# Fixed PSUM banks in the attention stage of a hybrid attention and Fourier block

## The chip, the cores and the metric

The kernel runs on one core of a Trainium2 chip. The metric is the device time of one execution in microseconds (us). The kernel before takes 612.53 us, the median of three runs (611.64, 612.53 and 614.63). The execution that was profiled took 611.92 us; its trace spans 610.1 us, and the other 1.8 us lie around the span.

## The reference

One layer of a backbone over 1024 latent tokens of width 1024, with 256 context tokens ahead of them as a prefix. One input projection feeds two groups: latent attention with 8 heads (low-rank queries and keys, a rotary part of 32), and a two-dimensional Fourier mixing followed by a linear map. The two are gated, concatenated and multiplied with one output matrix; a layer norm closes the layer. Cut to what matters here:

```python
h_x = _layer_norm(x) * (1.0 + scale_x) + shift_x
qlat_x, ckv_x, krope_x, gmla_x, fin_x, gf_x = _split_proj(h_x, w_in, b_in)
# per head (8 heads, 1024 queries, 1280 keys, 96 wide; values 64 wide)
s = einsum("bqhd,bkhd->bhqk", q, k) / sqrt(QK_DIM)
p = softmax(s, axis=-1)
attn_x = einsum("bhqk,bkhv->bqhv", p, v)
four_x = fft2(fin_x, axes=(1, 3)).real @ w_fourier + b_fourier
y = concatenate([attn_x * silu(g_mla), four_x * silu(g_f)]) @ w_out + b_out
x_new = _layer_norm(DEEPNORM_ALPHA * x + gate_x * y, post_ln_g, post_ln_b)
```

## The kernel before

The span has three parts. Up to about 283 us TensorE (PE) does the input projection, the query and key preparation and the Fourier transform. From 283 to about 505 us the attention loop runs, and from there to 602 us the output product with the layer norm behind it; the last 8 us are the layer norm's end.

Numbers are kept in two pieces, a high and a low one, so a product is three matmuls (h times h, h times l, l times h), and each tile that is read out of PSUM is read twice: ACT copies the high piece (`evac`, L774), and DVE subtracts it from the PSUM value to get the low piece (L776, L778). The PSUM bank is free only after the DVE readout.

The attention works on 32 pairs of 128-row query tiles (8 heads, 4 pairs each), a pair in about 7 us. Iteration n of the loop does the scores of pair n+1 (PE into SL0, SL1 and SC), their row minimum (DVE, E), the exponential (ACT, E), the split into a high (ACT, L1046) and a low piece (POOL, L1054; together EH), and the DMA transpose of both (ET<-EH), and for the pair of two iterations earlier the products with V (`pv`, PE, L1096 and L1099). The product is read out by ACT (pvt, L1105) and DVE (at, L1115). On all engines the loop's order is written out (SEQ). "f" in SEQ is a slot for a filling task of that iteration: building queries of the next head (`build_qt`, tile qh), keys (`build_kt`, kt), values (`build_v`, v), or the finish of two heads: `finish_rows` spreads the reciprocals of the row sums over 64 columns on POOL (rb, L1134), and `finish_pair` transposes them on PE (r, L1142) and scales the gate with them on DVE. `S0a` and `S0b` are parts of the scores, `P0` and `P1` the halves of the products with V. The last pairs transpose their weights on PE instead (et, `e_tr` and `e_out`).

PSUM has eight banks here: SL0 and SL1 take two each, SC one, and three rotate under the name "tr" for all that `tr(...)` allocates: qh, kt, v, r, pv, et and o. A new tile takes the bank of the oldest and waits for its readout.

In the output stage tiles t = 0 to 7 of 128 rows are accumulated over 8 blocks k; t = 0 and 1 (and 4, 5) go into SL0 and SL1, the others into SC and "tr" tiles (`po_t`: o20, o2512, o3, o60, ...; o70 is the first half of tile 7). `out_mms` issues the matmuls (L1193), and `finish` (DVE) multiplies with the gate (y, L1401), adds the residual (xr, L1402), takes the statistics (L1403, L1405), and scales (L1417, L1421). Outside the loop a scheduler orders the instructions of each engine when the program is built.

Of the kernel before, what the change touches and what calls it, by code (L numbers as in the profile page):

```python
# [11 lines left out]
F32 = mybir.dt.float32  # L12
# [7 lines left out]
PSUM = bass.MemoryType.PSUM  # L20

P = 128
# [30 lines left out]
FT = eval("{'k': [-1, 0, 1], 'q': [1, 2], 'r': 4, 'p': [6, 7], 'v': [13, 15, 15, 16, 17], 'g': 33}")  # L53
# [11 lines left out]
def tile_hybrid_block(ctx: ExitStack, tc: tile.TileContext, a, out, dbg=None):  # L65
# [11 lines left out]

    pools = {}

    def tr(name):  # L80
        return pools["tr"].tile([P, 512], F32, tag="tr", name=name)

    def split(hi, lo, src, eng=None):
        nc.gpsimd.tensor_scalar(out=hi, in0=src, scalar1=1.0, scalar2=0.0, op0=ALU.mult, op1=ALU.add)
        (eng or nc.vector).tensor_tensor(out=lo, in0=src, in1=hi.bitcast(F32), op=ALU.subtract)

    rest = []

    def hi_v(hi, lo, src):
# [616 lines left out]
    with tc.manual_schedule(engines={ET.PE}):  # L706
# [5 lines left out]
        pt = tr("cktc")  # L712
# [93 lines left out]

    V = {}

    def build_v(grp, i2, pool):
        if grp == 0 and i2 % 2 == 0:  # L810
            V[grp, i2 // 2] = u4([P, 2, 2, 4, 2, 64], F16, f"V{grp}{i2}")
        elif i2 == 0:
            v = qpool.tile([P, 5, 2, 4, 2, 64], F16, tag="q", name="V1")
            for i in range(0, 5, 2):
                V[grp, i // 2] = v[:, i:min(i + 2, 5)]
        pt = tr(f"v{grp}{i2}")
        for i in range(2):
            mm3(pt[:, 256 * i:256 * i + 256],
                [(ck(2 * i2 + i, 0), ck(2 * i2 + i, 1), wv[:, 0, 256 * grp:256 * grp + 256],
                  wv[:, 1, 256 * grp:256 * grp + 256])])  # L820
        vt = V[grp, i2 // 2][:, i2 % 2].rearrange("p i h l c -> p (i h) l c")
        evac(vt[:, :, 0, :], vt[:, :, 1, :], pt.rearrange("p (a c) -> p a c", c=64), pool)
# [39 lines left out]
    for par in range(2):  # L862
        pq = []
        for nt in range(4):
# [4 lines left out]
            if par == 1:  # L869
                t = u4([P, 2, 2, 4, 64], F32R, f"pqs{par}{nt}")  # L870
            else:
                if nt % 2 == 0:
                    t2 = pools["e"].tile([P, 2, 2, 2, 4, 64], F32R, tag="ET", name=f"pqs{par}{nt}", bufs=ETB)
                t = t2[:, nt % 2]
            pv = ps.rearrange("p (g t c) -> p t g c", t=2, c=64)
# [75 lines left out]
    def fourier_out(par, m, alloc):  # L951

        AT, BT, NT_ = four[par]
        NK = (258, 256)[par]
        ms = slice(m * P, (m + 1) * P)
        pa, pb = alloc(f"pa{par}{m}"), alloc(f"pb{par}{m}")
        nc.tensor.matmul(pa[:, 0:NK], lhsT=wn[:, 0, ms], rhs=NT_[:, 0:NK], start=True, stop=False)
        mm3(pa[:, 0:NK], [(wp_hi[:, gp, ms], wp_lo[:, gp, ms], AT[:, gp, 0, :], AT[:, gp, 1, :])
                          for gp in range(2)], False)
        mm3(pb[:, 0:NK], [(wm_hi[:, gp, ms], wm_lo[:, gp, ms], BT[:, gp, 0, :], BT[:, gp, 1, :])  # L960
                          for gp in range(2)])
        ta = small.tile([P, 512], F32, tag="h", name="ta", bufs=4)
        nc.scalar.activation(out=ta[:, 0:NK], in_=pa[:, 0:NK], func=AF.Identity, bias=bfo[:, m:m + 1])
        mf = mixf[m]
        if par == 0:
            outs = ((slice(0, 513, 2), 0, 257, ALU.subtract), (slice(1022, 512, -2), 1, 256, ALU.add))
        else:
            outs = ((slice(1, 512, 2), 0, 256, ALU.subtract), (slice(1023, 512, -2), 0, 256, ALU.add))
        for ks, r0, r1, op in outs:
            tf = small.tile([P, 512], F32, tag="h", name="tf", bufs=4)  # L970
            nc.vector.tensor_tensor(out=tf[:, r0:r1], in0=ta[:, r0:r1], in1=pb[:, r0:r1], op=op)
            nc.gpsimd.tensor_tensor(out=mf[:, ks], in0=tf[:, r0:r1], in1=mf[:, ks], op=ALU.mult)
        return ta
# [8 lines left out]
    ps_ctx.close()  # L982
    tr_ctx.close()
    at_ctx = ExitStack()
    pools["tr"] = at_ctx.enter_context(tc.tile_pool(name="ps_tr2", bufs=3, space=PSUM, reuse_waits="tile"))
    ps_s = at_ctx.enter_context(tc.tile_pool(name="ps_s", bufs=1, space=PSUM, reuse_waits="tile"))


# [1 line left out]
    SC = ps_s.tile([P, 512], F32, tag="SC", name="SC")  # L990

    class Pair:
# [91 lines left out]

        def pv(self, kts, first=False, last=False):
            if first:
                self.po = tr("pv")
            po = self.po[:, 0:256]
            tiles = self.ET.rearrange("p j t q -> p (j t) q")
            for hl in range(2):  # L1090
                for kt in kts:
                    v = V[self.grp, kt // 4][:, kt // 2 % 2, kt % 2, self.h % 4]
                    t, d = 10 * hl + kt, 20
                    e = tiles[:, t:t + d + 1:d, :]
                    if hl == 0:
                        nc.tensor.matmul(po, lhsT=v.rearrange("p l c -> p (l c)"), rhs=e, start=(kt == 0), stop=False)  # L1096
                    else:
                        g = kt % 2
                        nc.tensor.matmul(po[64 * g:64 * g + 64], lhsT=v[:, 0], rhs=e, start=False,  # L1099
                                         stop=(kt >= 8), tile_position=(0, 64 * g))  # L1100
# [25 lines left out]
    def finish_rows(pair, half):  # L1126

        rb = small.tile([P, 4, 2, 64], F32, tag="h", name="rb", bufs=4)
        for e in range(2):
            o, i = rb[:, :, e, :], rinv[2 * pair + e][:, 4 * half:4 * half + 4].unsqueeze(2).to_broadcast([P, 4, 64])  # L1130
            if RBE == "a":
                nc.scalar.activation(out=o, in_=i, func=AF.Copy)
            else:
                nc.gpsimd.tensor_scalar(out=o, in0=i, scalar1=1.0, scalar2=0.0, op0=ALU.mult, op1=ALU.add)  # L1134
        rbs[pair, half] = rb

    def finish_pair(pair, half):
        hs = slice(512 * half, 512 * half + 512)
        rb = rbs[pair, half]
        pt = tr(f"r{pair}{half}")  # L1140
        for i in range(4):
            nc.tensor.transpose(pt[:, i * P:(i + 1) * P], rb[:, i].rearrange("p a b -> p (a b)"), ident)  # L1142

        def out():
            nc.vector.scalar_tensor_tensor(out=gm[pair][:, hs], in0=pt, scalar=vscale[:, 0, pair:pair + 1],
                                           in1=gm[pair][:, hs], op0=ALU.mult, op1=ALU.mult)
            {'v': nc.vector, 'p': nc.gpsimd}[GME].tensor_tensor(out=gm[pair][:, hs], in0=ats[pair][:, hs], in1=gm[pair][:, hs], op=ALU.mult)

        on_dve(out)
# [34 lines left out]
    HALVES = ((0, 512), (512, 1024))  # L1184
# [11 lines left out]
    def po_t(t):  # L1196

        if t % 4 < 2:
            return {c: SL[t % 4][:, c[0]:c[1]] for c in HALVES}
        if t % 4 == 2:  # L1200
            return {c: tr(f"o{t}{c[0]}") for c in HALVES}
        return {HALVES[0]: SC, HALVES[1]: tr(f"o{t}")}

    NP = 4 * HEADS
    fills = {n: [] for n in range(NP + LAG)}
# [1 line left out]
    for h in range(HEADS - 1):  # L1207
        if h % 2:
            for c in range(3):
                fills[4 * h + FT['k'][c]].append(lambda c=c, p=(h + 1) // 2: build_kt(p, c, BP))  # L1210
        for hf in range(2):
            fills[4 * h + FT['q'][hf]].append(lambda hf=hf, h1=h + 1: build_qt(h1, hf, BQ))
        if h % 2:
            p = h // 2
            fills[4 * h + FT['r']].append(lambda p=p: (finish_rows(p, 0), finish_rows(p, 1)))
            for hf in range(2):
                fills[4 * h + FT['p'][hf]].append(lambda hf=hf, p=p: finish_pair(p, hf))
    for i, n in enumerate(FT['v']):
        fills[n].append(lambda i=i: build_v(1, i, BV))
# [18 lines left out]
    with tc.manual_schedule(engines={ET.PE}):  # L1238
        VA, VB = eval('(1,3)')
        for i2 in range(VA):  # L1240
            build_v(0, i2, False)
        p0.s_lat(0, 0)
        p0.s_lat(0, 1)
        p0.s_lat(0, 2)
        for i2 in range(VA, VB):
            build_v(0, i2, False)
        if "m0'" not in SEQ:
            p0.max_lat(0)
        if "c0'" not in SEQ:
            p0.max_ctx(0)  # L1250
        if "t0'" not in SEQ:
            p0.bias(0)
        if "x0'" not in SEQ:
            p0.exp(0)
        if "h0'" not in SEQ and not p0.on_pe(0):
            p0.hi(0)
        if "l0'" not in SEQ and not p0.on_pe(0):
            p0.lo(0)
        p0.s_lat(1, 0)
        p0.s_lat(1, 1)  # L1260
        p0.s_lat(1, 2)
        for i2 in range(VB, 3):
            build_v(0, i2, False)
        if "m1'" not in SEQ:
            p0.max_lat(1)
        if "c1'" not in SEQ:
            p0.max_ctx(1)
        if "t1'" not in SEQ:
            p0.bias(1)
        if "x1'" not in SEQ:  # L1270
            p0.exp(1)
        if "h1'" not in SEQ:
            p0.hi(1)
        if "l1'" not in SEQ:
            p0.lo(1)
        for m in range(2, 4):
            fourier_out(1, m, tr)
    for m in range(4):
        dump(f"mixf{m}", mixf[m])

    with tc.manual_schedule(engines={{'P': ET.PE, 'V': ET.DVE, 'A': ET.Activation, 'G': ET.Pool, 'S': ET.SP}[c] for c in MAN}):
        for n in range(NP + LAG):
            nxt, prv = pairs.get(n + 1), pairs.get(n - LAG)
            h = n // 4
# [233 lines left out]
```

## Time and profile before

| what | value |
|---|---|
| median of three runs | 612.53 us |
| profiled execution; its span | 611.92 us; 610.1 us |
| PE, DVE, ACT, POOL busy | 577.2, 384.4, 310.0, 280.9 us |
| PE's weight loads (PEld) busy | 461.1 us |
| chain that ended last | PE 59%, DMA 14%, DVE 8%, ACT 7%, POOL 4% of the span |

PE is busy for 95% of the span, but matmuls are pipelined and their ends in the trace are modelled, so that figure doesn't say that PE is at its peak. The chain that ended last follows the work back from the last instruction, at each step to what released it. Its shares say which waits matter in which stage; an engine that waits off that chain costs nothing.

### The profile page before, as it was taken

How to read it: one execution, taken by the hardware profiler on the slowest of the kernel's cores; microseconds unless marked ns; L12 is line 12 of the kernel's file. 1: busy time of each engine (PE TensorE's matmuls, PEld its weight loads, DVE VectorE, ACT ScalarE, POOL GpSimd, SP SyncE). 2: the span in 40 equal slices, each digit the busy share in tenths (PEclk: the TensorE clock that was granted, in tenths of full speed). 3: DMA queues.
4: the chain of work that ended last, by engine and by line, in shares of the span. 5: the costliest groups of instructions: out<-in, count | busy, mean ns of one | idle time of the engine just before them, and what ended most of it. 6: DMA issues, size and time to landing. Idle time of an engine off the chain costs nothing.

```text
span 610.1 us, 9587 instructions
## 1 busy us (share of the span) xinstructions
PE 577.2 (95%) x3521; PEld 461.1 (76%) x3521; DVE 384.4 (63%) x878; ACT 310.0 (51%) x484; POOL 280.9 (46%) x220
## 2 busy tenths in 40 slices
PE   8999999999999999999899999999889998999994
PEld 7787777888899999889666676776656666788883
DVE  6438317811003496687776778677757756699897
ACT  3323621211024343467999989889978875600000
POOL 3123215011002349665877887788998851400000
PEclk9999999999999999999999999999999999999998
DMA  9999029000001041212999999999999996520432
GB/s 287 317 307 397 28 70 319 15 1 0 1 0 53 1 130 46 71 44 44 181 194 187 202 184 176 185 173 207 193 180 193 192 214 209 219 92 0 154 123 105
DMA packets 191927, 86.86 MB, mean 142 GB/s; under 512 B 160428, under 2 KB 182188, under 8 KB 191880
## 3 DMA queue, kind: packets, MB, share of 16 engines
q1 hardware_dynamic: 191880, 86.24, 60.4%
q8 instruction: 28, 0.46, 0.3%
q14 instruction: 19, 0.16, 0.1%
HBM read 41.39 MB, written 4.20 MB: 75 GB/s over the span
## 4 chain that ended last, share of the span: by engine, by line
PE 59%; DMA 14%; DVE 8%; ACT 7%; issue 5%; POOL 4%; SPq 2%; DVEq 0%; POOLq 0%; ACTq 0%
DMA ET<-EH 12%; PE g L322 11%; PE SL L1193 7%; PE fin L322 7%; PE o L1193 5%; POOL EH L1054 3%; ACT EH L1046 3%; PE tm L137 2%; PE tm L138 2%; PE tm L139 2%; ACT E L1037 2%; PE pv L1096 2%; DVE E L1018 2%; PE pv L1099 2%; DMA wada<-in_w_ada_dram 1%
## 5 line engine op out<-in xcount | busy, mean ns | idle before, releaser
L1054 POOL TENSOR_TENSOR EH<-E,EH 128x1280 f16<-128x1280 f32 x61 | 160.3, 2633 | 39.4 <-ACT EH L1046 38.2
L1018 DVE TENSOR_SCALAR_CACHE_REDUCE E<-SL 128x1024 f32<-128x1024 f32 x64 | 78.1, 1221 | 24.6 <-POOL EH L1054 20.5
L1046 ACT ACTIVATE EH<-E 128x1280 f16<-128x1280 f32 x61 | 77.4, 1269 | 21.2 <-DMA ET<-EH 20.0
L1037 ACT ACTIVATE E<-E,mx 128x1280 f32<-128x1280 f32 x64 | 86.8, 1356 | 1.5 <-DVE mx L1031 0.9
L322 PE MATMUL fin<-h,wh 128*128 128x512 f32 x192 | 65.0, 406 | 0.0
L322 PE MATMUL g<-h,wh 128*128 128x512 f32 x192 | 60.3, 394 | 1.0 <-DVE upm L384 1.0
L1096 PE MATMUL pv<-ET,V 128*128 128x256 f16 x320 | 45.8, 274 | 14.3 <-DMA ET<-EH 9.4
L137 PE MATMUL SL<-KTh,QT 96*128 96x512 f32 x128 | 55.4, 433 | 0.5 <-ACT QT L774 0.5
L1096 PEld LDWEIGHTS <-V 128*128 128x128 f16 x320 | 26.8, 97 | 36.1 <-issue 26.8
L139 PE MATMUL SL<-KTh,QT 96*128 96x512 f32 x128 | 50.6, 395 | 0.0
L138 PE MATMUL SL<-KTl,QT 96*128 96x512 f32 x128 | 50.4, 394 | 0.0
L322 PEld LDWEIGHTS fin<-h,wh 128*128 128x128 f32 x192 | 35.9, 188 | 10.3 <-issue 2.9
L1018 DVE TENSOR_SCALAR_CACHE_REDUCE E<-SC 128x256 f32<-128x256 f32 x64 | 26.8, 419 | 26.7 <-PE SC L139 26.2
L322 PEld LDWEIGHTS g<-h,wh 128*128 128x128 f32 x192 | 36.0, 188 | 9.8 <-issue 1.4
L353 POOL TENSOR_SCALAR h<-xnT,mod 128x512 f32<-128x512 f32 x15 | 12.8, 854 | 62.4 <-DVE mod L272 29.7
L322 PE MATMUL g<-h,wl 128*128 128x512 f32 x96 | 37.8, 394 | 0.0
L322 PE MATMUL fin<-h,wl 128*128 128x512 f32 x96 | 37.1, 395 | 0.0
L113 ACT ACTIVATE rs_t<-mvf,eps 128x1 f32<-128x1 f32 x8 | 2.4, 295 | 68.1 <-DVE mvf L1405 61.6
L431 ACT ACTIVATE gt<-g,cols 128x512 f32<-128x512 f32 x12 | 8.0, 688 | 56.1 <-PE g L322 56.1
L1415 POOL TENSOR_TENSOR xr<-xr,lng 128x256 f32<-128x256 f32 x2 | 1.4, 726 | 70.7 <-ACT xr L1414 70.7
L1099 PE MATMUL pv<-ET,V 128*64 128x256 f16 x320 | 33.0, 282 | 0.0
L354 DVE TENSOR_TENSOR h<-h,h 128x512 fp32r<-128x512 f32 x15 | 13.6, 905 | 30.0 <-POOL h L353 22.7
(347 smaller groups left out, 1443.4 us busy)
## 6 DMA issues: line engine op xcount, KB each, us to landing
wada<-in_w_ada_dram SPq DMA_DIRECT2D x32, 256.0 KB, 6.0
x<-in_x_dram SPq DMA_DIRECT2D x8, 512.0 KB
wgate<-in_w_ada_dram SPq DMA_DIRECT2D x8, 512.0 KB, 7.5
wor<-in_w_out_dram SPq DMA_DIRECT2D x8, 512.0 KB, 4.0
xr<-in_x_dram SPq DMA_DIRECT2D x8, 512.0 KB, 4.3
out_dram<-xr SPq DMA_DIRECT2D x15, 256.0 KB, 2.1
wr<-in_w_in_dram SPq DMA_DIRECT2D x6, 512.0 KB, 5.4
wtr<-in_w_in_dram SPq DMA_DIRECT2D x4, 416.0 KB, 6.3
```

Of the source, the lines that this page charges most:

```text
L137: nc.tensor.matmul(ps, lhsT=sh, rhs=mh, start=(start and i == 0), stop=False)
L138: nc.tensor.matmul(ps, lhsT=sh, rhs=ml, start=False, stop=False)
L139: nc.tensor.matmul(ps, lhsT=sl, rhs=mh, start=False, stop=(i == n - 1))
L322: nc.tensor.matmul(ps, lhsT=(w.hi, w.lo, w.hi)[p][k][:, cs], rhs=h[:, p // 2], start=(k == 0 and p == 0), stop=(k == 7 and p == 2))
L354: nc.vector.tensor_tensor(out=hh[:, 1], in0=h, in1=hh[:, 0].bitcast(F32), op=ALU.subtract)
L1018: nc.vector.tensor_scalar(out=dst, in0=src, scalar1=0.0, scalar2=3e38, op0=ALU.add, op1=ALU.min, accum_out=self.mx[:, c:c + 1])
L1037: nc.scalar.activation(out=self.E[j], in_=self.E[j], func=AF.Exp, scale=-1.0, bias=self.mx[:, j:j + 1], accum_out=sums[self.h][:, qt:qt + 1])
L1046: nc.scalar.activation(out=o, in_=i, func=AF.Copy)
L1054: {"v": nc.vector, "p": nc.gpsimd}[eng].tensor_tensor(out=self.EH[j][:, 1, cs], in0=self.E[j][:, cs], in1=self.EH[j][:, 0, cs], op=ALU.sub ...
L1096: nc.tensor.matmul(po, lhsT=v.rearrange("p l c -> p (l c)"), rhs=e, start=(kt == 0), stop=False)
L1099: nc.tensor.matmul(po[64 * g:64 * g + 64], lhsT=v[:, 0], rhs=e, start=False, stop=(kt >= 8), tile_position=(0, 64 * g))
L1193: nc.tensor.matmul(ps[c], lhsT=st, rhs=w[:, c[0]:c[1]], start=(i == 0 and st is mh and w is wh), stop=(i == 7 and st is ml))
```

## The change

Of the three rotating banks, one is taken out and given to the products with V alone (tag "pv"); two rotate for the rest. In the output stage that bank also takes o3, which is half of tile 3; in the startup it takes v01 and the tiles pa12 and pa13. And the two halves of `finish_rows` no longer run in one iteration but in two that follow each other.

```diff
-    def tr(name):
-        return pools["tr"].tile([P, 512], F32, tag="tr", name=name)
+    def tr(name, tag="tr"):
+        return pools["tr"].tile([P, 512], F32, tag=tag, name=name, bufs=NBANKS[tag])
+
+    def pv_bank(name):
+        return tr(name, "pv")
...
+    NBANKS = {"tr": 3}
...
-    pools["tr"] = at_ctx.enter_context(tc.tile_pool(name="ps_tr2", bufs=3, space=PSUM, reuse_waits="tile"))
+    pools["tr"] = at_ctx.enter_context(tc.tile_pool(name="ps_tr2", bufs=2, space=PSUM, reuse_waits="tile"))
+    NBANKS.update(tr=2, pv=1)
...
             if first:
-                self.po = tr("pv")
+                self.po = pv_bank("pv")
...
-        return {HALVES[0]: SC, HALVES[1]: tr(f"o{t}")}
+        return {HALVES[0]: SC, HALVES[1]: pv_bank(f"o{t}")}
...
-            fills[4 * h + FT['r']].append(lambda p=p: (finish_rows(p, 0), finish_rows(p, 1)))
             for hf in range(2):
+                fills[4 * h + FT['r'] + hf].append(lambda hf=hf, p=p: finish_rows(p, hf))
                 fills[4 * h + FT['p'][hf]].append(lambda hf=hf, p=p: finish_pair(p, hf))
...
-            build_v(0, i2, False)
+            build_v(0, i2, False, (tr, pv_bank)[i2 % 2])
...
-        fourier_out(1, m, tr)
+        fourier_out(1, m, lambda name: tr(name, "pv" if name[:2] == "pa" else "tr"))
```

The banks also move the order where the scheduler decides it, and the task that now stands in the first filling slot moves the order in the loop. Behind the change all line numbers of the output stage are higher by five.

The first place is TensorE at the start of the output stage, behind the last transposes of the row sums (r31); o20 and o3 are halves of tiles 2 and 3, and wo, m are the matrices of a block k. Before:

```order
L1142 MATMUL r31_5261<-ident_70,rb_5148 128x128 x4
L1193 MATMUL SC_2686<-woh7_5207,ml7_5212 128x512
L1193 MATMUL o20_5317<-woh4_4267,mh4_4421 128x512
L1193 MATMUL o20_5317<-wol4_4268,mh4_4421 128x512
L1193 MATMUL o20_5317<-woh4_4267,ml4_4422 128x512
L1193 MATMUL o20_5317<-woh5_5110,mh5_5139 128x512
```

The same place after:

```order
L1147 MATMUL r31_5261<-ident_70,rb_5148 128x128 x4
L1198 MATMUL SC_2686<-woh7_5207,ml7_5212 128x512
L1198 MATMUL o3_5499<-woh4_4267,mh4_4421 128x512
L1198 MATMUL o3_5499<-wol4_4268,mh4_4421 128x512
L1198 MATMUL o3_5499<-woh4_4267,ml4_4422 128x512
L1198 MATMUL o3_5499<-woh5_5110,mh5_5139 128x512
```

Twelve matmuls of o3 now run ahead of o20. Before, one of those twelve ran before SL0's last matmul and eleven behind it, so SL0's last matmul now comes eleven matmuls later.

The second place is DVE at the end, around tile 7 (y, xr7, bnf; o70, SC and SL0 hold its three column pieces, and xr6 is tile 6). Before:

```order
L1421 SCALAR_TENSOR_TENSOR xr6_5778<-xr6_5778,rsf_5792,lnb_5315 128x512 x2
L1401 TENSOR_TENSOR y_5891<-SL0_2684,gate_5251 128x256
L1402 TENSOR_TENSOR xr7_5879<-y_5891,xr7_5879 128x256
L1403 BN_STATS bnf_5882<-xr7_5879 128x6
L1405 BN_AGGR mvf_5895<-bnf_5882 128x2
```

The same place after:

```order
L1406 TENSOR_TENSOR y_5883<-o70_5806,gate_5251 128x512
L1406 TENSOR_TENSOR y_5887<-SC_2686,gate_5251 128x256
L121 SCALAR_TENSOR_TENSOR rs_t_5794<-rsf_5792,rs_v_5793 128x1
L1406 TENSOR_TENSOR y_5891<-SL0_2684,gate_5251 128x256
L1407 TENSOR_TENSOR xr7_5879<-y_5883,xr7_5879 128x512
L1407 TENSOR_TENSOR xr7_5879<-y_5887,xr7_5879 128x256
L125 SCALAR_TENSOR_TENSOR rsf_5792<-rs_t_5794,rsf_5792 128x1
L1407 TENSOR_TENSOR xr7_5879<-y_5891,xr7_5879 128x256
L1408 BN_STATS bnf_5882<-xr7_5879 128x6 x2
L1426 SCALAR_TENSOR_TENSOR xr6_5778<-xr6_5778,rsf_5792,lnb_5315 128x512 x2
L1408 BN_STATS bnf_5882<-xr7_5879 128x6
L1410 BN_AGGR mvf_5895<-bnf_5882 128x2
```

All three pieces of tile 7 are now worked on behind the readout of SL0, and the scaling of tile 6 stands between them and the aggregate; before, two short instructions stood there.

The third place is TensorE at the end; o70 is written into a rotating bank. Before:

```order
L1193 MATMUL o6512_5729<-woh3_5302,ml3_5307 128x512
L1193 MATMUL o70_5806<-woh4_4267,mh4_4421 128x512
L1193 MATMUL o70_5806<-wol4_4268,mh4_4421 128x512
```

The same place after:

```order
L1198 MATMUL SC_2686<-woh3_5302,ml3_5307 128x256
L1198 MATMUL SL0_2684<-woh4_4267,mh4_4421 128x256
L1198 MATMUL SL0_2684<-wol4_4268,mh4_4421 128x256
L1198 MATMUL SL0_2684<-woh4_4267,ml4_4422 128x256
L1198 MATMUL SL0_2684<-woh5_5110,mh5_5139 128x256
L1198 MATMUL SL0_2684<-wol5_5111,mh5_5139 128x256
L1198 MATMUL o70_5806<-woh4_4267,mh4_4421 128x512
L1198 MATMUL o70_5806<-wol4_4268,mh4_4421 128x512
```

Where o70 came ahead of SC and SL0, it now comes behind all of SC and five matmuls of SL0.

## Rows read from the trace of the kernel before

**Rows 1.** Windows: start:end, us, busy PE, PEld, DVE, ACT, POOL (xcount), PEclk, DMA, GB/s.

```profile
350.00:380.00 30.00, 28.69 (x189) 20.50 (x188) 22.98 (x57) 27.38 (x39) 23.76 (x11) 1.00 1.04 181
557.00:595.00 38.00, 38.00 (x166) 30.88 (x165) 36.10 (x79) 1.18 (x4) 0.00 (x0) 1.00 0.32 111
```

**Rows 2.** Chain that ended last, around 340: start, us, what.

```profile
337.34 1.11 POOL rb L1134 x3
...
341.06 5.08 DMA ET<-EH
```

**Rows 3.** Timeline of POOL there: start, us, what, [idle before, releaser].

```profile
336.93 1.52 POOL L1134 TENSOR_SCALAR rb<-ri 128x256 f32<-128x256 f32 x4
...
344.10 2.63 POOL L1054 TENSOR_TENSOR EH<-E,EH 128x1280 f16<-128x1280 f32 x1 [0.47 <-ACT EH L1046]
```

**Rows 4.** Timeline of PE and DVE, pairs 7 and 28.

```profile
342.36 0.43 DVE L1115 TENSOR_TENSOR at<-pv,pvt 64x256 f32<-64x256 f32 x1
342.66 0.40 PE L1096 MATMUL pv<-ET,V 128*128 128x256 f16 x2
...
492.41 0.41 DVE L1115 TENSOR_TENSOR at<-pv,pvt 64x256 f32<-64x256 f32 x1
492.65 0.38 PE L1096 MATMUL pv<-ET,V 128*128 128x256 f16 x2
```

**Rows 5.** Timeline around pair 12.

```profile
377.33 0.64 PE L829 MATMUL qh<-ident,q_sb 128*96 128x128 f32 x4
...
378.43 0.69 DVE L778 SCALAR_TENSOR_TENSOR QT<-qh,QT 96x512 fp32r<-96x512 f32 x1 [0.56 <-ACT QT L774]
...
379.17 0.38 PE L1096 MATMUL pv<-ET,V 128*128 128x256 f16 x2 [0.50 <-DVE QT L778]
```

**Rows 6.** Timeline around pair 16.

```profile
406.46 0.60 PE L1142 MATMUL r<-ident,rb 128*128 128x128 f32 x4
...
407.60 0.39 PE L1096 MATMUL pv<-ET,V 128*128 128x256 f16 x2
407.67 0.68 DVE L776 TENSOR_TENSOR V<-v,V 128x512 f16<-128x512 f32 x1
```

**Rows 7.** Chain that ended last, around pair 16.

```profile
405.18 6.82 DMA ET<-EH
```

**Rows 8.** Timeline of the end of the attention.

```profile
507.93 0.38 PE L1073 MATMUL et<-ident,E 128*128 128x128 f32 x2
...
508.45 1.62 DVE L1083 TENSOR_TENSOR ET<-et,ET 128x512 f16<-128x512 f32 x3
508.62 1.05 ACT L102 ACTIVATE mh<-gt 128x1024 fp32r<-128x1024 f32 x1
...
509.73 0.50 PE L1193 MATMUL SL<-woh,mh 128*128 128x512 f32 x1 [1.42 <-ACT mh L102]
```

**Rows 9.** Chain that ended last, start of the output stage.

```profile
526.06 5.59 PE o L1193 x24
```

**Rows 10.** Timeline of DVE there.

```profile
545.78 0.69 DVE L1401 TENSOR_TENSOR y<-SL,gate 128x512 f32<-128x512 f32 x1 [0.16 <-PE SL L1193]
```

**Rows 11.** Timeline of PE and DVE at the end.

```profile
589.66 1.29 DVE L1401 TENSOR_TENSOR y<-o,gate 128x512 f32<-128x512 f32 x2
590.99 1.29 DVE L1402 TENSOR_TENSOR xr<-y,xr 128x512 f32<-128x512 f32 x2
592.27 1.28 DVE L1403 BATCH_NORM_STATS2 bnf<-xr 128x6 f32<-128x512 f32 x2
...
600.81 0.28 PE L1193 MATMUL SL<-woh,ml 128*128 128x256 f32 x1
```

**Rows 12.** Chain that ended last, at the end.

```profile
599.76 0.07 DVE rsf L121
...
600.22 1.31 DVE xr L1421 x2
601.54 0.35 DVE y L1401
...
602.83 0.25 DVE mvf L1405
```

More of the change, by code (lines that the diff above doesn't have):

```diff
@@ L807, in tile_hybrid_block, with build_v @@
     V = {}
-    def build_v(grp, i2, pool):
+    def build_v(grp, i2, pool, alloc=tr):
         if grp == 0 and i2 % 2 == 0:
@@ L815, in build_v @@
                 V[grp, i // 2] = v[:, i:min(i + 2, 5)]
-        pt = tr(f"v{grp}{i2}")
+        pt = alloc(f"v{grp}{i2}")
         for i in range(2):
```

## The prediction

> **What bounds the kernel now.** I read the windows first, since the share of busy time differs from stage to stage. In the attention loop PE is busy for 28.69 of 30 us, ACT for 27.38, POOL for 23.76, and the DMA engines all the time [rows 1]; nothing has much room, so the chain of waits must say who comes last. That chain runs through the DMA transposes ET<-EH and what feeds them (ACT's and POOL's EH, one piece of it POOL's rb) [rows 2], and in other pairs through PE and DVE. In the output stage PE is busy for all of 38 us and DVE for 36.10 [rows 1]: PE sets the pace, DVE follows with 1.9 us to spare. At the end DVE is alone with the layer norm of tile 7 [rows 12]. So the reader is to ask three things: what a wait for a bank costs in a loop bound by turns by DMA and by PE, what it costs at the loop's end where PE waits, and what another order costs on DVE at the end.
>
> **The change part by part.** First the loop. Taken out: a third bank for qh, kt, v and r, and for pv the right to take whichever bank is free. Added: pv(n) always waits for the readout at(n-1), since both have the one bank. The trace shows how often that is new. In seven of the 31 pairs (7, 11, 14, 19, 21, 23, 28) PE starts pv before the DVE readout of the pair before has ended: in pair 7 at 342.66 against 342.36+0.43 = 342.79, 0.13 too early, in pair 28 at 492.65 against 492.82, 0.17 too early [rows 4]. With about 0.06 for the signal, the seven come to 2.5 us. Three of them (11, 19, 28) lie on PE pieces of the chain, and they come to 0.7; the other four lie beside a DMA transpose of 5 us [rows 2], which hides them. Behind the waiting pv on PE stand the scores of the next pair, and for them waits DVE.
>
> With two banks, a fill waits for the fill before the last. In pair 12 qh41 starts at 377.33 while DVE reads its forerunner until 378.43+0.69 = 379.12 [rows 5]. It now starts at 379.17, and pv of pair 12 stands behind it with a third of the scores between them: I put these two at 1.15 (qh's row gives 0.64 with its overlap [rows 5], the three score matmuls make up the rest), so pv starts at 380.3 in place of 379.17, +1.15. The old wait of that pv (0.50 for DVE's QT) goes, but it ended at that same 379.17, so nothing comes back. In pair 16 the move of `finish_rows` pushes qh50 from the first slot of its iteration to the end, with v14 behind it; r10, now at 406.46, must wait for the readout of qh50, which takes the place of the readout of v at 407.67 to 408.35 [rows 6]. Then r10 starts at about 408.35 and pv at 408.35 + (407.60 - 406.46) = 409.5, +1.9. But a DMA of 6.82 us is what the chain follows there [rows 7], and it covers a part: I take 1.0, bounds 0 and 1.9.
>
> The split of rb gives something back. Four rb take 1.52 us on POOL ahead of an EH [rows 3], and 1.11 of them are on the chain [rows 2]. Two and two put half of that, 0.76, ahead of this EH and half ahead of the next, where POOL is idle for 0.47 us waiting for ACT [rows 3]. At three places (337, 395, 454) that is 2.3 at most; where POOL's wait covers only 0.47 of the 0.76, and the third place is on PE, less. I take -1.5. Loop: 0.7 + 1.15 + 1.0 - 1.5 = +1.3; bounds -2.3 (the gain alone) and 2.5 + 1.15 + 1.9 = +5.6 (every wait, no gain). In the startup v01, pa12 and pa13 have other banks, and qh10 waits 1.3 us longer, but the first pv waits for its DMA behind them: nothing.
>
> Second, the loop's end. The third tile of et in the last iteration starts at 507.93; it now takes the bank of the first, and waits for the first of the three DVE readouts that begin at 508.45 (1.62 for three, 0.54 each) [rows 8]: 509.0 plus the signal and what stands ahead, 509.2. ACT reads that tile just before mh (508.62, 1.05) in its order, and PE's matmul with mh waits for ACT, 1.42 us even now, to 509.73 [rows 8]. All of it moves by 509.2 - 507.93 = 1.3, to 511.0. I found no idle PE behind it until 545 that could take it back: +1.3, bounds 0 and 1.3.
>
> Third, the output stage, where the order changes. Behind r31 PE runs twelve o3 ahead of o20, eleven more ahead of SL0's last matmul than before, each 5.59/24 = 0.233 [rows 9]: SL0 is complete 2.55 later. DVE waits for it with its first readout, 0.16 now [rows 10]. It stands idle 2.55 longer, and what it did in that time comes later: the scaling of tiles 4 and 5, four instructions (1.31 for two [rows 12], so 2.6), now behind the readout of tile 6 that started at 589.66 [rows 11]. So DVE reaches the end full. There o70 has a rotating bank that waits for that same readout, so PE puts it behind SC and five matmuls of SL0, and DVE takes all three pieces of tile 7 behind the last one. PE itself ends as before, at 600.81+0.28 = 601.09 [rows 11]; DVE's work from 589.66 to its last readout, with the four instructions, adds up to about 11.0 against 11.4, so PE still decides, barely, and that readout starts at 601.13 and not at 601.54 [rows 12], 0.4 earlier. But behind it, before the aggregate at 602.83 [rows 12], there now stand one more addition of 512 columns (1.29/2 = 0.64) and of 256 (0.32, half of it), one more statistic of 512 (1.28/2 = 0.64) and of 256 (0.32) [rows 11], the rsf (0.07) and the scaling of tile 6 (1.31) [rows 12]: 3.3. 3.3 - 0.4 = +2.9. From the aggregate on the chain is as it was, about 7.3 us. Bounds: 0 if DVE had the time anyway, and 2.9 + 2.55 - 1.9 = 3.6 if the late start of DVE isn't made up but for its spare 1.9 [rows 1].
>
> Sum: 1.3 + 1.3 + 2.9 = +5.5. The profiled execution took 611.92 us, so 617.4; it lies 0.6 below the median of the runs, 612.53, on which the result is read, so 618.0.
>
> **A rule weighed.** On PE the windows give 28.69 of 30 us as busy, but its weight loads 20.50 [rows 1]. The Trainium skill says, in "Trainium Kernel Development and Optimization", section "Performance Expectations", that the busy share of matmuls misleads because they are pipelined, and that the busy share of LDWEIGHTS is the better measure. By it PE has a third of room in the loop and could take back the waits; it is the mechanism of the first rival. A rule speaks against the change: "Perfetto Trace Analysis", section "Matmul Optimizations", asks that all eight PSUM banks be used for parallelism. A bank with one owner stands empty between its uses; that mechanism is the second rival.
>
> **The rivals.** R1, not slower: the transposes set the loop's pace, PE takes back every wait for a bank, and the relief of POOL passes whole. For it: the chain of a DMA of 5 us behind rb [rows 2] and the room in PE's weight loads [rows 1]; against it: pv already waits for DVE's readout on the chain [rows 5]. Price: -2.3 + 1.3 + 2.9 = +1.9, 614.4; it decides as soon as less than about 1 us of the PE waits stays. If besides the loop's end is covered, 613.1.
>
> R2, every wait counts: with two banks each fill and each pv is in line with a readout, and none of it is hidden, since ACT at 27.38 of 30 [rows 1] can't catch up. 5.6 + 1.3 + 2.9 = +9.8, 622.3. Against it: four of the seven late pairs lie under a DMA.
>
> R3, the output stage costs nothing: DVE has the time to do the scaling of tiles 4 to 6 before the last readouts, as before. +2.6, 615.1. Against it: the order on DVE is fixed when the program is built, and it has the scaling behind.
>
> R4, the change works as a relief: pv never finds its bank taken by a fill, other waits shorten that I did not price, and the loop gains more than the 2.3. 610 or below. I see only one pair in which pv waits for a fill's readout [rows 5].
>
> **How the numbers follow.** Forecast 0.48, R1 0.20, R2 0.14, R3 0.12, R4 0.06. 0.5% of 612.5 is 3.1 us, about what a measurement of this kernel can tell from no change, so "same" ends at 615.6. R4 holds most of faster, 0.06. R1 and half of R3, with little from the forecast, are the same: 0.24. The rest is slower, 0.70. The forecast's own range is 616 to 620.5. The whole range leaves R4, and half of R2: 613.0 to 621.5.
>
> **What would show it.** In the profile after: a POOL line of rb x2 at each of six places; qh41 with idle time before it and a releaser DVE; the third et at about 509.2 and the wait for mh until about 511; DVE's idle time for SL0 at 545 of some 2.5 in place of 0.16; and from the last readout of SL0 to the aggregate 4.6 in place of 1.3. The prediction is wrong if the span of the loop (first pv to the last scores) shrinks by over 1 us, or if the aggregate still follows the last readout within 2 us.

## The result and the profile after

The changed kernel takes 617.55 us (median of four, 617.1 to 617.95) where the kernel before takes 612.46 beside it: a ratio of 1.0077 of the means, 95% interval 1.005 to 1.0105, so it is slower by about 5 us. 618.0 was forecast. A second measurement gave 1.0095 (1.0071 to 1.012). The profiled execution has a span of 616.1 us, 6.0 more than before.

PE is nearly in the same place at the first product with V (294.55 against 294.31), so the loss lies behind it. (From the first keys, kt, to that product it takes 28.21 us in the three profiles with three rotating banks and 28.34 to 28.39 in the nine of changed kernels, so the startup costs 0.15.) I cut the rest at four marks that every kernel here has: the first pv, the pv of pair 28, the first r of the last heads on PE, and the aggregate of tile 7 on DVE.

| us | loop (pv of pair 0 to 28) | its end (pv of 28 to r) | output stage (r to aggregate) |
|---|---|---|---|
| before | 198.34 | 32.14 | 78.04 |
| changed | 198.91 | 34.60 | 80.73 |
| difference | +0.6 | +2.5 | +2.7 |

The output stage first. The first readout of SL0 on the timeline of DVE in the changed kernel answers to [rows 10]:

```profile
551.57 0.69 DVE L1406 TENSOR_TENSOR y<-SL,gate 128x512 f32<-128x512 f32 x1 [2.69 <-PE SL L1198]
```

DVE is idle 2.69 us for it, 0.16 before. The chain that ended last, in the changed kernel's last stretch, answers to [rows 12]:

```profile
602.15 2.25 PE SL L1198 x19
604.40 0.02 issue
604.42 0.42 DVE y L1406
604.85 0.93 DVE xr L1407 x2
605.78 0.07 DVE rsf L125
605.85 0.34 DVE xr L1407
606.18 0.93 DVE bnf L1408 x2
607.11 1.31 DVE xr L1426 x2
608.42 0.35 DVE bnf L1408
608.77 0.02 issue
608.79 0.25 DVE mvf L1410
```

The last readout waits for PE (SL0, 604.40), not for DVE, as forecast; three additions, three statistics and the scaling of tile 6 stand between it and the aggregate, 4.37 us where there were 1.29.

At the loop's end, the timeline of the changed kernel answers to [rows 8]:

```profile
509.21 1.29 DVE L1088 TENSOR_TENSOR ET<-et,ET 128x512 f16<-128x512 f32 x2
509.96 0.44 PE L1078 MATMUL et<-ident,E 128*128 128x128 f32 x2 [1.10 <-DVE ET L1088]
510.72 1.05 ACT L106 ACTIVATE mh<-gt 128x1024 fp32r<-128x1024 f32 x1
511.82 1.22 PE L1198 MATMUL SL<-woh,mh 128*128 128x512 f32 x2 [1.42 <-ACT mh L106]
512.83 0.63 PE L1198 MATMUL SL<-wol,mh 128*128 128x512 f32 x1
```

The third transposed tile now waits 1.10 us for the readout of the first, and ACT's mh and PE's matmul move with it. But the matmul itself is slow: 1.22 us for two, 0.73 elsewhere. The windows of the changed kernel say why; the column behind POOL's is the granted clock:

```profile
510.00:512.00 2.00, 0.58 (x3) 0.35 (x4) 1.13 (x3) 1.56 (x3) 0.00 (x0) 0.82 1.00 392
512.00:514.00 2.00, 2.00 (x5) 1.61 (x6) 2.00 (x3) 1.65 (x2) 0.78 (x1) 0.50 0.04 15
514.00:516.00 2.00, 2.00 (x8) 1.57 (x8) 1.56 (x2) 0.00 (x0) 2.00 (x3) 0.82 0.00 0
```

For some 3 us TensorE ran at half speed, 1.2 GHz in place of 2.4; in the 2 us in which the clock fell it was busy for 0.58. The profile before shows 1.00 there, and the forecast had nothing of it.

In the loop the waits came where they were forecast. Pair 12 and pair 16 on PE's timeline of the changed kernel, answering to [rows 5, 6]:

```profile
379.25 0.64 PE L833 MATMUL qh<-ident,q_sb 128*96 128x128 f32 x4 [1.57 <-DVE QT L782]
...
380.44 0.72 PE L1101 MATMUL pv<-ET,V 128*128 128x256 f16 x5
...
408.18 0.63 PE L1147 MATMUL r<-ident,rb 128*128 128x128 f32 x4 [1.38 <-DVE QT L782]
...
409.35 0.72 PE L1101 MATMUL pv<-ET,V 128*128 128x256 f16 x5
```

The two pv start 1.27 and 1.75 us later than before (1.15 and 1.9 were forecast); 0.24 of each was there at the first pv already. And yet the loop as a whole is only 0.6 longer: at pair 22 the changed kernel is 0.19 ahead (452.07 against 452.26). What became of it is in PE's waits from 295 to 500 us (us in all, times, longest; the largest rows, of 13.7 us in all before and 14.7 after). Before:

```profile
PE pv L1096 <- DMA ET<-EH: 8.1, 10, 2.3
PE pv L1096 <- DVE E L1018: 2.0, 3, 0.7
PE pv L1096 <- DVE at L1115: 1.8, 2, 1.0
```

Changed:

```profile
PE pv L1101 <- DVE at L1120: 5.5, 7, 1.2
PE pv L1101 <- DMA ET<-EH: 3.3, 4, 1.1
PE pv L1101 <- DVE E L1023: 1.7, 2, 1.1
PE qh L833 <- DVE QT L782: 1.6, 1, 1.6
PE r L1147 <- DVE QT L782: 1.4, 1, 1.4
```

The waits for the banks (5.5, 1.6 and 1.4) took the place of waits for the transposes (8.1 to 3.3) and of other readouts: PE waits for its own readouts first, and by then the data is there.

And the split of rb on POOL's timeline of the changed kernel, against [rows 3]: two and two now stand ahead of two EH, as forecast (at one of the six places, 394, as two single ones with idle time between).

```profile
337.30 0.77 POOL L1139 TENSOR_SCALAR rb<-ri 128x256 f32<-128x256 f32 x2
338.04 2.63 POOL L1059 TENSOR_TENSOR EH<-E,EH 128x1280 f16<-128x1280 f32 x1
...
343.84 0.77 POOL L1139 TENSOR_SCALAR rb<-ri 128x256 f32<-128x256 f32 x2
344.58 2.63 POOL L1059 TENSOR_TENSOR EH<-E,EH 128x1280 f16<-128x1280 f32 x1
```

### The profile page after: what moved, and what is told of

It reads as the page before. It is cut to its first block, busy times and chain, and to the rows that moved or that the text cites. A ratio compares the mean times of both kernels' runs of the same rounds, so it can differ in the third digit from the quotient of the medians.

```text
span 616.1 us, 9577 instructions
## 1 busy us (share of the span) xinstructions
PE 578.8 (94%) x3521; PEld 463.1 (75%) x3521; DVE 384.2 (62%) x878; ACT 310.3 (50%) x484; POOL 280.6 (46%) x220
## 4 chain that ended last, share of the span: by engine, by line
PE 64%; DMA 13%; DVE 6%; ACT 6%; POOL 5%; issue 4%; SPq 1%; DVEq 0%; POOLq 0%; ACTq 0%
PE g L326 11%; DMA ET<-EH 11%; PE SL L1198 7%; PE fin L326 7%; PE o L1198 5%; POOL EH L1059 4%; PE pv L1101 3%; PE tm L141 2%; PE tm L142 2%; PE tm L143 2%; ACT EH L1051 2%; PE pv L1104 2%; PE SL L141 2%; ACT E L1042 2%; PE SL L143 2%
```

## The experiments

My theory was that the 6 us are a term at the loop's end and two terms in the output stage (the late SL0, the late o70), and that the loop itself hardly counts. Each experiment takes one of these away or leaves one part alone. Ratios are to the kernel before, run beside it. The marks above make the kernels comparable across chips, since one execution differs from another by up to 2.0 us before any of the changed code begins (the first kt starts between 265.96 and 267.95). Each kernel has one profile, and the eight with the changed kernel's loop (all but the last three rows, and the changed kernel itself) have loops of 197.54 to 199.00, so a difference of under 1.5 us in that column shows nothing by itself.

| kernel | ratio (95%) | loop | its end | output stage |
|---|---|---|---|---|
| changed, again | 1.0095 (1.0071 to 1.012) | 198.51 | 33.31 | 80.73 |
| output banks as before | 1.0022 (1.0011 to 1.0033) | 198.86 | 34.84 | 78.09 |
| o70 moved alone | 1.0062 (1.004 to 1.0084) | 197.54 | 33.30 | 79.68 |
| stage's start alone | 1.0062 (1.0046 to 1.0079) | 198.80 | 34.69 | 79.37 |
| third et tile moved | 1.0041 (1.0027 to 1.0055) | 198.98 | 32.13 | 80.73 |
| eight transposes added | 1.0065 (1.0048 to 1.0082) | 198.19 | 34.86 | 80.73 |
| output and et | 1.0002 (0.9987 to 1.0018) | 199.00 | 32.13 | 78.09 |
| rows in one round | 1.0091 (1.0068 to 1.0113) | 199.09 | 34.85 | 80.74 |
| before with the split | 0.9987 (0.9971 to 1.0004) | 196.90 | 32.17 | 78.09 |
| before, split, queries kept | 0.9979 (0.9966 to 0.9992) | 196.97 | 32.16 | 78.20 |

**The output stage's banks as before.** o20 and o60 take the pv bank, o3 a rotating one.

```diff
-            return {c: tr(f"o{t}{c[0]}") for c in HALVES}
-        return {HALVES[0]: SC, HALVES[1]: pv_bank(f"o{t}")}
+            return {c: (pv_bank, tr)[c[0] > 0](f"o{t}{c[0]}") for c in HALVES}
+        return {HALVES[0]: SC, HALVES[1]: tr(f"o{t}")}
```

> The changed kernel with the output stage's banks dealt as before (o20 and o60 take the bank of the products with V, o2512, o3, o6512 and o70 the two others); the order on PE and DVE there is then that of before, the loop and its end stay changed. Theory: the output stage cost 2.7 us (aggregate of tile 7 at 608.79 against 602.83, less the 3.27 that PE was late at r), so 617.55 - 2.7 = 614.9, DVE's first readout of SL0 idle under 0.3 us in place of 2.69, and from the readout of SL0 to the aggregate 1.3 us in place of 4.4. Rival (the end of the chain is set by PE, late by 3.3 us in any case, and the rest by the spread of the runs): 617 to 618.

The output stage is back at 78.09 us. The timeline of DVE, without idle time at SL0, and two lines of the chain at the end, of this kernel:

```profile
549.95 1.29 DVE L1406 TENSOR_TENSOR y<-SL,gate 128x512 f32<-128x512 f32 x2
```

```profile
605.78 0.35 DVE y L1406
...
607.07 0.25 DVE mvf L1410
```

The readout is followed by the aggregate after 1.29 us again, as before. 1.0022 is 3.4 us below the changed kernel's 1.0077; 2.7 were expected, and the marks give 2.64. The other 0.7 stay unexplained, inside the two intervals. Only bank names were changed, and the scheduler put the order back. The rival is out.

**o70 moved alone.**

```diff
-                  (tr("o70"), SC[:, 0:256], SL[0][:, 0:256])))
+                  (pv_bank("o70"), SC[:, 0:256], SL[0][:, 0:256])))
```

> The changed kernel with o70 in the bank of the products with V, so that PE does it ahead of SC and SL0 again; o3 is still ahead of o20 at the start. Theory: two things add up in the output stage, DVE's late first readout and the late o70; this takes away the second alone. DVE is still idle 2.7 us before SL0, has the scaling of tile 6 behind its last readout, and the aggregate follows that readout by 3.2 us (4.4 in the changed kernel, 1.3 before): 1.1 us less, 616.4. Rival (the place of o70 is all): 2.7 less, 614.9.

The timeline of DVE, and the chain at the end, of this kernel:

```profile
550.15 1.29 DVE L1406 TENSOR_TENSOR y<-SL,gate 128x512 f32<-128x512 f32 x2 [2.69 <-PE SL L1198]
```

```profile
605.10 1.31 DVE xr L1426 x2
606.41 0.16 DVE mvf L1410
```

DVE's idle 2.69 us are still there and the scaling of tile 6 still stands ahead of the aggregate; the stage gave back 1.05 (80.73 to 79.68), 1.1 expected. By the stage the rival (all of it) is out. The ratio is 0.9 us lower than the changed kernel's first one, inside its interval; the marks decide here.

**The stage's start alone.** The other term: o20 in the pv bank and o3 in a rotating one, o70 still behind o60.

```diff
-            return {c: tr(f"o{t}{c[0]}") for c in HALVES}
-        return {HALVES[0]: SC, HALVES[1]: pv_bank(f"o{t}")}
+            return {c: (pv_bank if t == 2 and c[0] == 0 else tr)(f"o{t}{c[0]}") for c in HALVES}
+        return {HALVES[0]: SC, HALVES[1]: tr(f"o{t}")}
```

> The changed kernel with the output stage's start dealt as before (o20 in the bank of the products with V, o3 in a rotating one), and o70 still in the bank whose last user is o60, so that PE still does it late. Theory: the output stage's 2.7 us are two terms, and this takes the other one than the kernel with o70 moved. DVE's idle time before SL0 falls from 2.7 to under 0.3, the scaling of tile 6 is done before the last readout, and from that readout to the aggregate it is 2.8 us (4.4 changed, 3.2 with o70 moved, 1.3 before): 1.7 less than the changed kernel, so +0.55% against before where the changed one has +0.8 to +0.95%. In its trace, from PE's r to the aggregate: 79.0 us (78.04 before, 80.73 changed). Rival (the late o70 is all): no gain.

The idle time is gone, as is the scaling from the end of the chain of this kernel:

```profile
605.49 0.42 DVE y L1406
605.91 1.27 DVE xr L1407 x3
607.18 1.27 DVE bnf L1408 x3
608.47 0.25 DVE mvf L1410
```

The stage is 79.37, 1.36 less than changed, 1.7 expected: counted from r, the last readout begins 0.36 before its place in the kernel before, and 2.98, not 2.8, pass to the aggregate. By the stage the rival (no gain) is out; the ratio, 1.0062 for 1.0055 expected, can't tell it from the changed kernel. The two terms taken apart give 1.05 + 1.36 = 2.4 of the 2.7; the rest comes back only when both are gone, as in the kernel with the banks as before.

**The third transposed tile moved.**

```diff
-            pt = self.pt[j, c] = tr("et")
+            pt = self.pt[j, c] = (pv_bank if (self.n, j, c) == (NP - 1, 1, 2) else tr)("et")
```

> The changed kernel with one tile moved: the third transposed tile of the last iteration takes the bank of the products with V, which is free since 507.3. No instruction changes place. Theory: the wait of 1.10 us before that tile goes, and with it PE's half clock from 511 to 515 (PEclk 0.82, 0.50, 0.82 in the windows of 2 us), so 1.3 + 1.2 = 2.5 us less, 615.05, and clock 1.00 in all these windows. Rival 1 (the clock falls whatever this wait is): 616.2, with the half clock still there. Rival 2 (the wait is taken back later): 617.5.

No instruction moved, the wait is gone, and the loop's end is 32.13, as before. The timeline of PE of this kernel:

```profile
508.82 0.38 PE L1078 MATMUL et<-ident,E 128*128 128x128 f32 x2
510.62 0.73 PE L1198 MATMUL SL<-woh,mh 128*128 128x512 f32 x2 [1.42 <-ACT mh L106]
```

The clock is 1.00 in all the windows there. So the bank's wait, with the half clock behind it, costs 2.5 us; rival 2 is out. Rival 1 is not settled by one profile: whether the half clock belongs to the wait is another question.

**Eight transposes added** into the idle time, which nobody reads; "W" stands ahead of the third tile's transposes in the written order of the last iteration.

```diff
+                elif c == "W":
+                    wt = pv_bank("wt")
+                    for i in range(8):
+                        nc.tensor.transpose(wt[:, i % 4 * P:i % 4 * P + P], ident, ident)
```

> The changed kernel with eight more transposes of the identity on PE, into the bank of the products with V (nobody reads them), just ahead of the third transposed tile of the last iteration, where PE is idle for 1.10 us. The wait stays: that tile still starts near 509.95 and the matmul with mh near 511.8. Theory: the half clock follows the longer idle time, so the clock stays at 1.00 and 1.2 us come back, 616.35. Rival (the half clock comes with the idle 1.42 us before mh, or by chance): unchanged, 617.5.

The timeline of PE, and two of the windows, of this kernel:

```profile
508.56 1.03 PE L1355 MATMUL wt<-ident 128*128 128x128 f32 x8
509.82 0.44 PE L1078 MATMUL et<-ident,E 128*128 128x128 f32 x2 [0.23 <-DVE ET L1088]
511.68 1.09 PE L1198 MATMUL SL<-woh,mh 128*128 128x512 f32 x2 [1.42 <-ACT mh L106]
```

```profile
512.00:514.00 2.00, 2.00 (x6) 1.51 (x6) 2.00 (x3) 1.52 (x2) 0.92 (x1) 0.50 0.17 66
514.00:516.00 2.00, 2.00 (x8) 1.58 (x7) 1.42 (x2) 0.00 (x0) 2.00 (x3) 0.68 0.04 8
```

The idle time fell from 1.10 to 0.23, and the half clock came all the same (34.86). (The ratio of 1.0065 would fit the theory's 616.35, but its interval holds the rival's 617.5 too; the trace decides.) And with o70 moved alone, where nothing differs at this place, it did not come. PE's timeline and a window of that kernel:

```profile
509.86 0.44 PE L1078 MATMUL et<-ident,E 128*128 128x128 f32 x2 [1.10 <-DVE ET L1088]
511.71 0.73 PE L1198 MATMUL SL<-woh,mh 128*128 128x512 f32 x2 [1.42 <-ACT mh L106]
```

```profile
512.00:514.00 2.00, 2.00 (x10) 1.60 (x10) 2.00 (x3) 1.56 (x2) 0.89 (x1) 1.00 0.09 33
```

So my theory of the idle time fell: the same wait goes with and without it. In the profiles with the wait (seven, the changed kernel twice) the loop's end is 33.3 us in two, without the half clock, and 34.6 to 34.9 in five; in the five without the wait (before, et moved, output and et, both splits) it is 32.1 to 32.2. The wait itself costs 1.15, the half clock 1.3 to 1.6 more when it comes. It never came here without the wait, so the wait may well be a condition, but not the only one. What brings it stays open; a filling of products in place of transposes was not tried.

**Output and et together** leaves the loop's changes alone (the two edits above).

> The changed kernel with the output stage's banks dealt as before and the third transposed tile of the last iteration in the bank of the products with V: what stays is the loop's own bank for pv, two for the fills, the split of rb and the queries that it pushes back. Theory: the loop alone costs 0.5 us, because its DMA transposes cover the waits of pairs 12 and 16 within six pairs, so +0.1% against before (0 to 0.25%). Rival (the waits of 1.6 and 1.4 us count as forecast, 1.3 us and more): +0.25 to 0.4%.

1.0002: the loop's changes together cost nothing that can be measured (1.1 us at most, by the interval), in spite of waits of 1.6 for qh and 1.4 for r in its profile. The rival is out; the slowdown sits behind the loop.

**The split alone, on the kernel before.** The loop, three rotating banks, with the last edit of the change.

> The kernel before with one part of the change alone: finish_rows in two iterations, which also pushes qh30, qh50 and qh70 to the end of theirs; three rotating banks as before. The forecast gave the split a gain of 1.5 us at most 2.3, and the pushed qh a loss of 0 to 1.9. Theory now: the loop absorbs both, 0.0 (-0.1 to +0.1%). Rival: the split's gain passes whole, -0.25% or better.

The loop is 196.90 against 198.34, 1.4 us shorter; the ratio is 0.9987, 0.8 us, with an interval that touches 1. "The loop absorbs both" is not what the profile says, and the rival's 1.5 is not what the time says; this run alone leaves both open, and the last experiment settles it. The kernel with output and et together has the same split, and differs by the banks of the loop and the startup alone: it is 2.1 us longer in the loop and 0.9 in the ratio, with intervals that overlap. So in the changed kernel the split's gain seems to stand against a cost of the banks.

**Rows in one round, on the changed kernel.**

> The changed kernel with finish_rows in one iteration again (four rb in a row on POOL, qh50 back in the first slot); banks as changed. Theory: the wait of r10 for the readout of qh50 (1.4 us) goes and pv of pair 16 starts about 1.2 us earlier, but both are absorbed by pair 24, so the time stays that of the changed kernel, +0.8%. Rival (the split's gain was real): 1.5 us more, +1.05%.

The loop is 199.09, 0.2 to 0.6 above the changed kernel's two and 0.75 above the kernel before; the ratio, 1.0091 against 1.0095 beside it, shows no difference. r10's wait is gone, pv of pair 16 follows that of pair 12 by 27.3 us in place of 28.9, and nothing comes of it. With the fixed banks the split is worth nothing that these runs can tell.

**The kernel before with the split, queries kept in place.** The second half takes the second filling slot.

```diff
-            fills[4 * h + FT['r']].append(lambda p=p: (finish_rows(p, 0), finish_rows(p, 1)))
+            fills[4 * h + FT['r']].append(lambda p=p: finish_rows(p, 0))
...
+    for h in range(1, HEADS - 1, 2):
+        fills[4 * h + FT['r'] + 1].append(lambda p=h // 2: finish_rows(p, 1))
```

> The kernel before with the row sums' broadcasts in two rounds and nothing else moved: the second half of finish_rows takes the second filling slot of its iteration, behind the queries, so qh30, qh50 and qh70 stay where they were; three rotating banks. Theory: the gain of the split in the loop (1.4 us in the profile of the split alone) comes without the queries' push, so 1.0 to 1.5 us less than before, -0.2%, and this beats both kernels. Rival (the pushed queries were the gain, not the split): 0.0.

0.9979 (0.9966 to 0.9992): 1.3 us faster than before, clear of no change, and with it faster than both kernels. The loop is as short as with the split alone (196.97 and 196.90). The rival is out: the split is the gain, not the pushed queries.

## Why the prediction was right

617.55 against 618.0, and slower as forecast. By its own steps:

- **The output stage, +2.9 forecast, +2.7 measured.** Shown: the readout of SL0 idle for 2.69 (2.55 + 0.16 forecast; eleven times 0.233 is 2.56), PE setting the last readout, 4.4 to the aggregate (4.6 forecast); and dealing these banks as before takes all of it away.
- **The loop's end, +1.3 forecast, +2.5 in the profile (+1.2 in the changed kernel's second).** The wait is 1.15 to 1.3, and moving one tile removes it. The half clock behind it, 1.3 to 1.6 in five of seven profiles, is a term the forecast lacked.
- **The loop, +1.3 forecast, +0.2 to +0.6 in the changed kernel's two profiles (-0.8 to +0.7 in all eight with this loop), and with it alone 1.0002.** The waits were right at their places to 0.4 us, counted from the first pv (1.03 and 1.51 for 1.15 and 1.9), but the price of passing them on was too high: I left 0.7 + 1.15 + 1.0 on the path, and by pair 22 all was made up, since PE would have waited for the transposes there anyway (8.1 us to 3.3). The split's -1.5 is what it gives with three banks (-1.4 of the loop, 1.3 in time), but with the fixed banks no run shows a gain of it: the two terms don't add, as the forecast had them do. That half of R1, PE's waits taken back, was true; its other half, the split's gain passing whole, was not.
- R2 (622.3), R3 (615.1) and R4 (610) are out: the loop passes little on, DVE's order does decide, and there is no gain beyond the forecast's.
- The startup, put at nothing, took 0.15. And the chances of R1 and half of R3 add up to 0.26, where the forecast has 0.24 for "same".

So the mechanisms of the loop's end and of the output stage were right; that the sum came out to half a microsecond is luck: the loop's price was about 0.7 to 1.1 too high and the end's 1.2 too low, and the half clock that made it so doesn't come in every execution.

On the rule that was weighed: the Trainium skill says, in "Trainium Kernel Development and Optimization", section "Performance Expectations", that matmul busy time is a bad metric of how close a kernel is to its limit and that the busy share of LDWEIGHTS is a good one. No run here tells the two apart: the loop took the waits back, but in place of PE's waits for the transposes, idle time that the matmuls' busy share shows as well (206.20 of 222 us from 283 to 505 before), and at the end, where there was no such idle time, 1.15 us stayed.

## What to carry to other kernels

A bank with a fixed owner changes more than the waits at its place: where a scheduler orders the rest, the name of a bank moved whole blocks of matmuls, and nearly half of the loss in the profiles came from there. Price a new wait at the next place where that engine would wait anyway: inside this loop, which waits for DMA, it was made up within ten pairs, though the gain of the split went with it; at the loop's end, with no wait behind it, it cost its full length. Try the parts of a change apart: the split alone, in a filling slot that moves nothing else, made the kernel before 0.2% faster.

## What the runs showed of the hardware

The half clock at the loop's end came in five of the seven profiles with the wait. The changed kernel and the one with o70 moved have the same instructions and waits there and the same busy shares ahead (PE busy 0.90 and 0.58 of 2 us); one had it and the other not. Filling most of the wait with transposes did not keep it away. Nor does it belong to this place: the kernel with the third transposed tile moved has it inside the loop (granted clock 0.50 from 454 to 456 us). Its pair 23 came 1.5 us later than before, counted from the first pv, and its pair 26 only 0.4 later, like the changed kernel's: the loop made up this delay of PE too.

The span's mean clock in the runs of the kernel before also varies, from 0.983 to 0.995, so such stretches belong to single executions. The kernel before was profiled at 0.995 and the changed one at 0.987, so some of the 6.0 us between the two profiles may be this. A mark in the trace told a term of 1 us better than the time of a run.
